# Attention with split operands in a mixed attention, recurrence and expert kernel

## The chip, the cores and the metric

The kernel runs on one core of one Trainium2 chip. The metric is device microseconds (us) of one execution. The engines are named as in the profile: PE (TensorE, matmuls), PEld (its weight loads, which overlap PE), DVE (VectorE), ACT (ScalarE), POOL (GpSimd) and SP (SyncE, which issues nearly all transfers).

## The reference

One layer over 1024 tokens of width 1024. Two mixers work on the same projected input, and a mixture of experts follows. What the change touches is the attention mixer (8 heads, keys of 64 + 32 dimensions, values of 64) and where the output of the other mixer, a recurrence, is kept.

```python
def causal_attention(q, k, v):                      # blocks of 128 queries
    scores = jnp.einsum('bqhd,bkhd->bhqk', qb, k, preferred_element_type=jnp.float32) * scale
    scores = jnp.where(k_pos[None, :] <= q_pos[:, None], scores, -jnp.inf)
    probs = jax.nn.softmax(scores, axis=-1).astype(v.dtype)
    return jnp.einsum('bhqk,bkhd->bqhd', probs, v)
...
    mla_o = mla_group(p[..., :MLA_IN], ...)         # attention, then an RMS norm
    rwkv_o, v_i = rwkv7_group(p[..., MLA_IN:], ...) # the recurrence
    mix = jnp.concatenate([mla_o, rwkv_o], axis=-1) @ w_o[i]
    x = layer_norm(DEEPNORM_ALPHA * x + (1.0 + gt1) * mix, ...)
    ffn = moe_ffn(h, ...)                           # 32 experts, top 4
```

All operands are float32.

## The kernel before

The program is one long list of instructions, laid out by a planner that simulates the time line and fixes the order of each engine's queue; every queue is then worked off in order. The stages follow one another, and the planner overlaps their edges.

1. **phase_a** normalizes and transposes the input. **phase_c** projects it, 18 blocks of 128 columns. Each block takes 16 matmul products in three passes: an operand x is kept as hi (x rounded to the format fp32r) and lo (x - hi), and `mm` (lines 187 to 195) adds hi·hi, hi·lo and lo·hi. `split` (line 202) makes the pair: ACT casts, DVE subtracts. In the second half of phase_c, for each p of 4, three recurrence blocks are projected (`shifted`), then the rotary part of the queries (`rotary`, every other p), the rest of queries and keys (`nope`) and two blocks of values. Each result goes from PSUM into a tile `stage` (three buffers of 128x1024) and from there by DMA into DRAM tensors q_d, k_d, kr_d, v_d and rkv_d. PSUM tiles of tag `sm` have four banks.
2. **mixers** interleaves 8 attention heads (`head`) with 8 recurrence units (`rwkv_unit`, two 64-wide heads and half the sequence each, in four stages). A head loads its queries Q (96x1024), keys K (96 rows) and, for two heads at a time, values `vp`; Q and K have two buffers, `vp` one. Then, for each block qb of 128 queries: one or two score products of up to 512 keys (line 889) in plain float32, a mask product (891), the maximum on DVE (892), the exponential on ACT (898), the division by the sum on ACT (902), transposes of the 128x128 blocks on PE (910), in groups of up to four into one PSUM bank `mt`, and a copy of each group into the tile `pt` (912: DVE for the first group, ACT for the second). Every second block, a product of the values with `pt` is put off until the next block's transposes (`pv`, lines 914 to 925): values are the stationary operand (128 keys x 64), `pt` the moving one (128 x 256), in plain float32; its result is in the same single bank `mt` and ACT copies it into oT. A plain float32 product is two matmul instructions in the trace.
   A unit ends with `self.dst[p][:, ts]` written by DVE (847), an SBUF tile that holds all recurrence outputs.
3. **mix** takes groups of 256 tokens: `mix_in` splits the recurrence output and the normalized attention output, `mix_mm` multiplies by w_o (recurrence rows 4 to 7 first), then come layer norm, router and gates. The tiles oT and dst are used again for the residual rows `y`.
4. **moe** runs 32 experts with streamed weights, all of them in split passes.

Of the kernel before, what the change touches and what calls it, by code (L numbers as in the profile page):

```python
# [10 lines left out]
F32 = mybir.dt.float32  # L11
# [8 lines left out]
P = 128  # L20
# [4 lines left out]
NH = 8  # L25
# [37 lines left out]
WBUF, SBUF = 5, 4  # L63
MODS = 2
# [97 lines left out]
class Build:  # L162
# [49 lines left out]
    def setup(self):  # L212
# [244 lines left out]
    def phase_c(self, st, keep, rw_stack):  # L457
# [54 lines left out]
        nc.sync.dma_start(self.kr_d, t1[0:32])  # L512
# [41 lines left out]
        def rotary(g):  # L554
# [21 lines left out]
        for p in range(4):  # L576
# [10 lines left out]
            for b in (2 * p, 2 * p + 1):  # L587
                pv = self.psum("sm", 4)
                self.mm(pv, kn[:, b * P:(b + 1) * P], uv)
                t = stage()[:, 0:512]  # L590
                S.copy(t, pv)
                nc.sync.dma_start(self.v_d[b], t)
            if p == EARLY_UNIT:
# [5 lines left out]
                self.unit(0)  # L599

# [56 lines left out]
    def rwkv_unit(self, u):  # L657
# [189 lines left out]
        V.tensor_mul(self.dst[p][:, ts], pg, o)  # L847
# [3 lines left out]
    def mla_setup(self, st):  # L851
# [3 lines left out]

        self.Q, self.K = ([kp.tile([P, T], F32, name=f"{n}{j}") for j in range(2)] for n in "QK")
        for t in self.Q + self.K:
            nc.gpsimd.memset(t[96:P], 0.0)
        for K in self.K:
            nc.sync.dma_start(K[64:96], self.kr_d)  # L860
# [5 lines left out]
        self.vp = None  # L866

    def head(self, h, oT):
# [4 lines left out]
        Q, K = self.Q[h % 2], self.K[h % 2]  # L873
        nc.sync.dma_start(Q[0:96], self.q_d[h])
        nc.sync.dma_start(K[0:64], self.k_d[h])
        if h % 2 == 0:
            self.vp = ap.tile([P, NB, P], F32, name="vp", bufs=1)
            nc.sync.dma_start(self.vp, self.v_d[:, :, h * 64:h * 64 + P].rearrange("b p c -> p b c"))
        v = self.vp[:, :, half]
        late = None  # L880
        for qb in range(NB):
            n = (qb + 1) * P
            ss, mx, sm = [], ap.tile([P, 2], F32, name="m"), ap.tile([P, 2], F32, name="smm")
            pr = ap.tile([P, T], F32, name="pr")
            for j, c in enumerate(range(0, n, 512)):
# [3 lines left out]
                mm(s, Q[:, qb * P:(qb + 1) * P], K[:, c:c + w], start=True, stop=not last)  # L889
# [14 lines left out]
            if i == 0:  # L904
                pt = ap.tile([P, NB, 256], F32, name="pt", bufs=2)
            for k0 in range(0, qb + 1, 4):
# [4 lines left out]
                eng = S.copy if k0 else V.tensor_copy  # L911
                eng(pt[:, k0:k1, i * P:(i + 1) * P], tp[:, 0:(k1 - k0) * P].rearrange("p (k q) -> p k q", q=P))

            def pv(nk=qb + 1, pt=pt, t=qb // 2):
                po = self.psum("mt", 1)
                if t == 0:
                    mm(po[half, 0:P], v[:, 0], pt[:, 0, 0:P], start=True, stop=True)
                    for k in range(2):
                        mm(po[half, P:256], v[:, k], pt[:, k, P:256], start=(k == 0), stop=(k == 1))
                else:  # L920

                    for k in [0, nk - 1] + list(range(1, nk - 1)):
                        sl = slice(P, 256) if k == nk - 1 else slice(0, 256)
                        mm(po[half, sl], v[:, k], pt[:, k, sl], start=(k == 0), stop=(k == nk - 2))
                S.copy(oT[half, t * 256:(t + 1) * 256], po[half, 0:256])
# [9 lines left out]
    def mixers(self, st, left, first, oT, dst):  # L935
# [4 lines left out]
        self.dst = dst  # L940
# [836 lines left out]
```

## Time and profile before

| | us |
|---|---|
| median of 3 runs | 2546.7 (2533.74 to 2546.89) |
| the profiled execution, its own time | 2529.01 |
| its span, first to last instruction | 2527.2 |
| PE busy in the span | 2316.8 (92%) |
| weight loads (PEld) busy | 1960.6 (78%) |
| DVE busy | 1991.1 (79%) |
| ACT busy | 1414.6 (56%) |
| POOL busy | 533.4 (21%) |
| mean granted TensorE clock | 0.953 of full speed |

Busy times are unions of instruction durations. A matmul's duration includes the time in which its pipeline fills and drains, so successive matmuls overlap, and PE can be "busy" while it takes in nothing new. How far apart matmuls start tells what one of them costs. Rows of waits give how long an engine sat idle before an instruction, and what ended that.

### The profile page before, as it was taken

Reading aid. Unit: us, or ns where it says so; the run is one execution under the profiler, and the core shown is the slowest. Engines: PE = TensorE matmul, PEld = TensorE weight load, DVE = VectorE, ACT = ScalarE, POOL = GpSimd, SP = SyncE. Lnnn points to the kernel's source line nnn. Section 1 sums busy time; section 2 is a strip of 40 time slices with the busy share of each in tenths; the row PEclk is TensorE's granted clock in tenths of the full one; section 3 lists DMA queues with packets and bytes.
Section 4 is the critical chain, followed back from the end, with each engine's and each line's share of the span. In section 5 each row is a group of like instructions: output and inputs, shape, how many; then the busy total and the mean of one; then the engine's idle time right before and its main releaser. Section 6 shows DMA issues by size and latency. Waiting matters only on the chain. (4 is left out here: it accounts for less than half of the span.)

```text
span 2527.2 us, 41955 instructions
## 1 busy us (share of the span) xinstructions
PE 2316.8 (92%) x15523; PEld 1960.6 (78%) x15523; DVE 1991.1 (79%) x3854; ACT 1414.6 (56%) x2357; POOL 533.4 (21%) x411
## 2 busy tenths in 40 slices
PE   6999989999999895999999999989999898989992
PEld 3777766776666784988988888989889888889981
DVE  7666456676765776987988888888979798888977
ACT  5333333454546233765766666666657576666764
POOL 1004222222213444110112121121202021211113
PEclk9999989999989995999999999999989999999996
DMA  6378542222112225976978878787969788887973
GB/s 261 117 255 287 178 108 49 52 48 66 43 37 80 98 87 195 347 290 232 341 284 304 316 285 332 283 304 276 346 225 336 281 304 300 291 309 289 326 275 148
DMA packets 167334, 567.79 MB, mean 225 GB/s; under 512 B 64617, under 2 KB 79738, under 8 KB 116821
## 3 DMA queue, kind: packets, MB, share of 16 engines
q1 hardware_dynamic: 155476, 524.63, 56.6%
q0 software_dynamic: 11216, 39.34, 6.0%
q8 instruction: 124, 2.03, 0.3%
q10 hardware_dynamic: 432, 1.09, 0.1%
q14 instruction: 86, 0.70, 0.1%
HBM read 508.22 MB, written 56.79 MB: 224 GB/s over the span
## 5 line engine op out<-in xcount | busy, mean ns | idle before, releaser
L204 DVE TENSOR_TENSOR wsl<-w,wsh 128x1024 fp32r<-128x1024 f32 x786 | 936.6, 1225 | 140.1 <-ACT wsh L203 139.0
L203 ACT CAST wsh<-w 128x1024 fp32r<-128x1024 f32 x786 | 782.6, 1047 | 337.5 <-PE acc L193 95.2
L1508 PE MATMUL acc<-xw,wsh 128*128 128x368 f32 (+7 forms) x1408 | 387.7, 359 | 19.0 <-DVE t L1513 11.1
L193 PE MATMUL acc<-wsh,xTl 128*128 128x256 f32 x1344 | 382.1, 285 | 0.3 <-DVE xTl L204 0.3
L191 PE MATMUL acc<-wsh,xTh 128*128 128x256 f32 x1344 | 381.1, 284 | 0.9 <-ACT xTh L203 0.9
L192 PE MATMUL acc<-wsl,xTh 128*128 128x256 f32 x1344 | 381.5, 284 | 0.0
L1510 PE MATMUL acc<-xw,wsl 128*128 128x184 f32 (+7 forms) x1408 | 341.5, 243 | 0.0
L1508 PEld LDWEIGHTS acc<-xw,wsh 128*128 128x128 f32 x1408 | 274.5, 195 | 22.6 <-issue 12.0
L1442 POOL DMA_INDIRECT y_d<-y,idx x42 | 132.1, 3146 | 710.0 <-DVE y L1434 612.5
L1510 PEld LDWEIGHTS acc<-xw,wsl 128*128 128x128 f32 x1408 | 279.0, 198 | 0.4
L192 PEld LDWEIGHTS acc<-wsl,xTh 128*128 128x128 f32 x1344 | 258.4, 192 | 3.8
L191 PEld LDWEIGHTS acc<-wsh,xTh 128*128 128x128 f32 x1344 | 258.3, 192 | 2.5 <-ACT xTh L203 1.3
L193 PEld LDWEIGHTS acc<-wsh,xTl 128*128 128x128 f32 x1344 | 258.2, 192 | 1.6 <-DVE xTl L204 0.8
L191 PE MATMUL acc<-wsh,uTh 128*128 128x512 f32 x512 | 203.2, 398 | 8.2 <-ACT uTh L203 8.2
L192 PE MATMUL acc<-wsl,uTh 128*128 128x512 f32 x512 | 202.7, 396 | 0.0
L193 PE MATMUL acc<-wsh,uTl 128*128 128x512 f32 x512 | 195.1, 406 | 0.9 <-DVE uTl L204 0.9
L1346 POOL DMA_INDIRECT xg<-h_d,idx x43 | 95.1, 2211 | 367.7 <-DVE gate L1338 232.6
L191 PE MATMUL sm<-hTh,wsh 128*128 128x512 f32 x288 | 116.5, 405 | 6.7 <-ACT wsh L203 2.0
L192 PE MATMUL sm<-hTl,wsh 128*128 128x512 f32 x288 | 117.1, 407 | 4.2 <-DVE hTl L345 3.1
L191 PEld LDWEIGHTS acc<-wsh,uTh 128*128 128x128 f32 x512 | 97.4, 191 | 29.4 <-ACT uTh L203 9.3
L193 PE MATMUL sm<-hTh,wsl 128*128 128x512 f32 x288 | 115.2, 400 | 0.0
L192 PEld LDWEIGHTS acc<-wsl,uTh 128*128 128x128 f32 x512 | 97.5, 190 | 18.9
(582 smaller groups left out, 4371.4 us busy)
## 6 DMA issues: line engine op xcount, KB each, us to landing
w<-in_w_dram SPq DMA_DIRECT2D x384, 1024.0 KB
aw<-in_ada_dram SPq DMA_DIRECT2D x34, 512.0 KB
w<-in_w_in_dram SPq DMA_DIRECT2D x18, 512.0 KB
aw<-in_ada_dram SPq DMA_DIRECT2D x7, 1024.0 KB
rkv_d<-stage SPq DMA_DIRECT2D x12, 512.0 KB
xt<-in_x_dram SPq DMA_DIRECT2D x8, 512.0 KB
xr<-in_x_dram SPq DMA_DIRECT2D x8, 512.0 KB
xr_d<-xr SPq DMA_DIRECT2D x8, 512.0 KB
```

Source lines behind the costliest of these rows:

```text
L191: mm(out, a.hi, b.hi, start=start, stop=False)
L192: mm(out, a.hi, b.lo, start=False, stop=False)
L193: mm(out, a.lo, b.hi, start=False, stop=stop)
L203: (hi_eng or self.nc.scalar.copy)(dst.hi, src)
L204: (lo_eng or self.nc.vector).tensor_tensor(dst.lo, src, dst.hi.bitcast(F32), ALU.subtract)
L1346: nc.gpsimd.indirect_dma_start(out=xg[0:n], out_offset=None, in_=self.h2_d, in_offset=bass.IndirectOffsetOnAxis(ap=idx[0:n, 0:1], axis=0))
L1442: nc.gpsimd.indirect_dma_start(out=self.y_d, out_offset=bass.IndirectOffsetOnAxis(ap=idx[0:n, 0:1], axis=0), in_=y[0:n], in_offset=None, c ...
L1508: nc.tensor.matmul(acc[:, 0:2 * cap], w.hi[:, c], xw[:, k].rearrange("p a t -> p (a t)"), start=(k == 0), stop=False)
L1510: nc.tensor.matmul(acc[:, 0:cap], w.lo[:, c], xw[:, k, 0], start=False, stop=(k == KD - 1))
```

## The change

- Queries, keys and values are written to DRAM as hi and lo parts: q_d, k_d and kr_d get a leading dimension of 2, and v_d rows become 1024 wide. phase_c makes the parts, with `parted` for the rotary results (in the two stage tiles already held) and `split` into two stage tiles in `nope`, and into one tile of full width for the values.
- In the values' layout each head has 128 columns, hi beside lo, with the order turned for odd heads so that hi lies at the head's own half.
- Scores are three fp32r products per chunk instead of one float32 product. Q and K are loaded per half sequence (two Q tiles, three K buffers), and the rotary key rows for each head anew.
- The transposed weights are split (ACT cast, DVE subtraction, both from PSUM) instead of copied. The product with the values uses one 128-column stationary operand with both parts of the values, and two moving passes, hi and lo; the two halves of the result are added at the end (ACT copies one half to `ol`, DVE adds).
- The recurrence output goes to a DRAM tensor ro_d, and `mix_in` loads 256 tokens of it for each group. The SBUF tile dst goes.

```diff
+KBUF = 3
...
-        self.q_d = dram("q_d", [NH, 96, T])
-        self.k_d = dram("k_d", [NH, 64, T])
-        self.kr_d = dram("kr_d", [32, T])
-        self.v_d = dram("v_d", [NB, P, 512])
+        self.q_d = dram("q_d", [2, NH, 96, T])
+        self.k_d = dram("k_d", [2, NH, 64, T])
+        self.kr_d = dram("kr_d", [2, 32, T])
+        self.v_d = dram("v_d", [NB, P, 1024])
+        self.ro_d = dram("ro_d", [4, P, T])
@@ phase_c
-        nc.sync.dma_start(self.kr_d, t1[0:32])
+        for part, t in enumerate(self.parted(t1[0:32], t2[0:32])):
+            nc.sync.dma_start(self.kr_d[part], t)
@@ rotary
-            for j in range(4):
-                nc.sync.dma_start(self.q_d[4 * g + j, 64:96], t1[32 * j:32 * j + 32])
+            for part, t in enumerate(self.parted(t1, t2)):
+                for j in range(4):
+                    nc.sync.dma_start(self.q_d[part, 4 * g + j, 64:96], t[32 * j:32 * j + 32])
@@ nope
-            t = stage()
-            for h, pq in enumerate(project(name, p * P, srcs)):
-                S.copy(t[:, halves[h]], pq)
-            for h in range(2):
-                nc.sync.dma_start(dst[2 * p + h, 0:64], t[h * 64:h * 64 + 64])
+            th, tl = stage(), stage()
+            for sl, pq in zip(halves, project(name, p * P, srcs)):
+                self.split(Split(th[:, sl].bitcast(F32R), tl[:, sl].bitcast(F32R)), pq)
+            for part, t in enumerate((th, tl)):
+                for h in range(2):
+                    nc.sync.dma_start(dst[part, 2 * p + h, 0:64], t[h * 64:h * 64 + 64])
@@ values
-                t = stage()[:, 0:512]
-                S.copy(t, pv)
+                t = stage()
+                t4 = t.bitcast(F32R).rearrange("p (a n d) -> p a n d", a=4, n=4)
+                self.split(Split(t4[:, :, 0::3], t4[:, :, 1:3]), pv.rearrange("p (a n d) -> p a n d", a=4, n=2))
                 nc.sync.dma_start(self.v_d[b], t)
@@
+    def parted(self, x, hi):
+        self.split(Split(hi.bitcast(F32R), x.bitcast(F32R)), x)
+        return hi, x
@@ rwkv_unit
-        V.tensor_mul(self.dst[p][:, ts], pg, o)
+        V.tensor_mul(o, pg, o)
+        nc.sync.dma_start(self.ro_d[p, :, ts], o)
@@ mla_setup: the tiles Q and K, the memsets of rows 96 to 128 and the load of kr_d go
@@ head
-        Q, K = self.Q[h % 2], self.K[h % 2]
-        nc.sync.dma_start(Q[0:96], self.q_d[h])
-        nc.sync.dma_start(K[0:64], self.k_d[h])
-        if h % 2 == 0:
-            self.vp = ap.tile([P, NB, P], F32, name="vp", bufs=1)
-            nc.sync.dma_start(self.vp, self.v_d[:, :, h * 64:h * 64 + P].rearrange("b p c -> p b c"))
-        v = self.vp[:, :, half]
+        other = slice(0, 64) if h % 2 else slice(64, 128)
+        parts = lambda d: d.rearrange("a r t -> r a t")
+        Q, K = [], []
+        for sl in (slice(0, 512), slice(512, T)):
+            q, k = (ap.tile([96, 2, 512], F32R, name=n, bufs=b) for n, b in (("Q", 2), ("K", KBUF)))
+            nc.sync.dma_start(q.bitcast(F32), parts(self.q_d[:, h, :, sl]))
+            nc.sync.dma_start(k[0:64].bitcast(F32), parts(self.k_d[:, h, :, sl]))
+            nc.sync.dma_start(k[64:96].bitcast(F32), parts(self.kr_d[:, :, sl]))
+            for t, ts in ((q, Q), (k, K)):
+                ts.append(Split(t[:, 0], t[:, 1]))
+        v = ap.tile([P, NB, P], F32R, name="vp", bufs=1)
+        nc.sync.dma_start(v.bitcast(F32), self.v_d[:, :, h * P:(h + 1) * P].rearrange("b p c -> p b c"))
...
-                mm(s, Q[:, qb * P:(qb + 1) * P], K[:, c:c + w], start=True, stop=not last)
+                q, k = Q[qb // 4][:, qb % 4 * P:(qb % 4 + 1) * P], K[j][:, 0:w]
+                mm(s, q.hi, k.hi, start=True, stop=False)
+                mm(s, q.hi, k.lo, start=False, stop=False)
+                mm(s, q.lo, k.hi, start=False, stop=not last)
...
-                pt = ap.tile([P, NB, 256], F32, name="pt", bufs=2)
+                pt = self.split_tile(ap, [P, 6 + qb % 4, 256], f"pt{qb % 4}", bufs=1)
...
-                eng = S.copy if k0 else V.tensor_copy
-                eng(pt[:, k0:k1, i * P:(i + 1) * P], tp[...])
+                self.split(pt[:, k0:k1, i * P:(i + 1) * P], tp[...])
             def pv(nk=qb + 1, pt=pt, t=qb // 2):
                 po = self.psum("mt", 1)
+                def prod(k, sl, start, stop):
+                    mm(po[:, sl], v[:, k], pt.hi[:, k, sl], start=start, stop=False)
+                    mm(po[:, sl], v[:, k], pt.lo[:, k, sl], start=False, stop=stop)
...
-                        mm(po[half, sl], v[:, k], pt[:, k, sl], start=(k == 0), stop=(k == nk - 2))
-                S.copy(oT[half, t * 256:(t + 1) * 256], po[half, 0:256])
+                        prod(k, slice(P, 256) if k == nk - 1 else slice(0, 256), k == 0, k == nk - 2)
+                ol = ap.tile([P, 256], F32, name="ol", bufs=1)
+                S.copy(ol[half], po[other, 0:256])
+                V.tensor_tensor(oT[half, t * 256:(t + 1) * 256], po[half, 0:256], ol[half], ALU.add)
@@ mix_in, with ro a tile of 128x4x256 for group 0 and a slice of the new tile ys for the others
+        self.nc.sync.dma_start(ro, self.ro_d[:, :, ts].rearrange("j p t -> p j t"))
         for j in range(4):
-            self.split(mt[4 + j], ro[j][:, ts])
+            self.split(mt[4 + j], ro[:, j])
```

## Rows read from the trace of the kernel before

**Rows 1.** Stages; each engine's busy us with (x) instructions, granted clock, DMA share.

```profile
core 0: us, PE busy (x) PEld busy (x) DVE busy (x) ACT busy (x) POOL busy (x), PEclk, DMA share, GB/s
...
190.00:342.00 152.00, 144.83 (x634) 112.67 (x632) 79.13 (x99) 54.99 (x86) 53.33 (x30) 0.99 0.62 213
342.00:400.00 58.00, 47.85 (x325) 33.46 (x326) 42.61 (x149) 24.44 (x58) 12.29 (x16) 0.82 0.39 93
400.00:690.00 290.00, 283.98 (x2527) 202.53 (x2527) 201.79 (x679) 145.79 (x337) 71.74 (x114) 0.97 0.21 49
690.00:816.00 126.00, 116.85 (x959) 79.23 (x957) 72.94 (x233) 61.93 (x140) 32.92 (x39) 0.93 0.19 52
...
985.00:2527.00 1542.00, 1413.94 (x9684) 1296.38 (x9684) 1336.21 (x2142) 992.59 (x1514) 268.24 (x108) 0.96 0.80 293
```

**Rows 2.** Time line of PE between two busy units: start, duration of the run.

```profile
565.68 1.73 PE L924 MATMUL mt<-pt,vp 128*64 128x256 f32 x8
567.34 0.88 PE L750 MATMUL s<-rx,bk 64*128 64x64 f32 x6
...
570.70 1.02 PE L686 MATMUL s<-wdad,a 64*128 64x512 f32 x2
571.56 0.77 PE L750 MATMUL s<-rx,bk 64*128 64x64 f32 x6
...
572.59 0.60 PE L910 MATMUL mt<-csts,pr 128*128 128x128 f32 x4
573.03 0.95 PE L624 MATMUL s<-csts,oc 128*128 128x2 f32 x8
```

**Rows 3.** Time line of PE in the experts, fp32r products.

```profile
1100.94 0.40 PE L1455 MATMUL acc<-bs,pick 128*128 128x512 f32 x1
1101.17 0.28 PE L191 MATMUL acc<-wsh,xTh 128*128 128x256 f32 x1
...
1103.93 0.28 PE L193 MATMUL acc<-wsh,xTl 128*128 128x256 f32 x1
```

**Rows 4.** Attention products by line: duration min/median/max ns, starts, forms.

```profile
L889 PE MATMUL ms<-K,Q x192: 275/592/1220, 349.0 to 792.1; 128*128 128x512 f32 x96, 128*128 128x128 f32 x32, 128*128 128x256 f32 x32, 128*128 128x384 f32 x32
...
L924 PE MATMUL mt<-pt,vp x288: 272/379/686, 377.1 to 809.9; 128*64 128x256 f32 x120, 128*64 128x128 f32 x24
...
L919 PE MATMUL mt<-pt,vp x32: 272/272/273, 366.6 to 779.4; 128*64 128x128 f32 x32
...
L917 PE MATMUL mt<-pt,vp x16: 272/274/323, 366.3 to 778.9; 128*64 128x128 f32 x16
```

**Rows 5.** Copies out of bank mt by line, duration min/median/max ns.

```profile
L912 DVE COPY pt<-mt x64: 275/676/692, 361.9 to 804.7; 128x512 f32<-128x512 f32 x40, 128x128 f32<-128x128 f32 x8, 128x256 f32<-128x256 f32 x8, 128x384 f32<-128x384 f32 x8
L912 ACT COPY pt<-mt x32: 266/419/587, 375.1 to 806.2; 128x128 f32<-128x128 f32 x8, 128x256 f32<-128x256 f32 x8, 128x384 f32<-128x384 f32 x8, 128x512 f32<-128x512 f32 x8
```

**Rows 6.** Groups by line: a split out of PSUM, weight loads of both widths.

```profile
L192 PEld LDWEIGHTS acc<-wsl,xTh 128*128 128x128 f32 x1344 | 258.4, 192 | 3.8
...
L924 PEld LDWEIGHTS mt<-pt,vp 128*64 128x64 f32 x288 | 37.0, 140 | 21.6 <-issue 3.5 <-ACT pt L912 1.5 <-ACT pr L898 0.8
...
L204 DVE TENSOR_TENSOR xTl<-tr,xTh 128x512 fp32r<-128x512 f32 x42 | 28.3, 683 | 42.6 <-ACT xTh L203 42.6
...
L203 ACT CAST xTh<-tr 128x512 fp32r<-128x512 f32 x42 | 24.2, 585 | 74.4 <-PE tr L1357 73.4
```

**Rows 7.** Waits in the mixers: total us, times, longest.

```profile
ACT pr L898 <- PE mt L910: 44.2, 21, 4.6
```

**Rows 8.** Waits in the late projections.

```profile
ACT stage L591 <- DMA q_d<-stage: 6.2, 3, 3.2
...
ACT stage L440 <- DMA v_d<-stage: 2.8, 1, 2.8
```

**Rows 9.** Time line of PE at the first scores.

```profile
348.95 2.90 PE L889 MATMUL ms<-K,Q 128*128 128x128 f32 x6 [3.41 <-DMA K<-k_d]
```

**Rows 10.** Time line at the start of the mix.

```profile
816.48 0.79 PE L191 MATMUL mm<-wo4h,mt4h 128*128 128x512 f32 x1 [2.78 <-ACT mt4h L203]
```

More of the change, by code (lines that the diff above doesn't have):

```diff
@@ L854, in mla_setup @@
         self.ap = self.pool(st, "ap", bufs=2, side="right")
[L856 to L860, printed above, removed]
         self.nmask = kp.tile([P, P], BF16, name="nmask")
@@ L882, in head @@
             n = (qb + 1) * P
-            ss, mx, sm = [], ap.tile([P, 2], F32, name="m"), ap.tile([P, 2], F32, name="smm")
+            ss, ms = [], ap.tile([P, 4], F32, name="m")
+            mx, sm = ms[:, 0:2], ms[:, 2:4]
             pr = ap.tile([P, T], F32, name="pr")
@@ L910, in head @@
                     nc.tensor.transpose(tp[:, (k - k0) * P:(k - k0 + 1) * P], pr[:, k * P:(k + 1) * P], self.ident)
[L911 to L912 removed]
+                self.split(pt[:, k0:k1, i * P:(i + 1) * P], tp[:, 0:(k1 - k0) * P].rearrange("p (k q) -> p k q", q=P))
             def pv(nk=qb + 1, pt=pt, t=qb // 2):
                 po = self.psum("mt", 1)
+                def prod(k, sl, start, stop):
+                    mm(po[:, sl], v[:, k], pt.hi[:, k, sl], start=start, stop=False)
+                    mm(po[:, sl], v[:, k], pt.lo[:, k, sl], start=False, stop=stop)
                 if t == 0:
[L917 removed]
+                    prod(0, slice(0, P), True, True)
                     for k in range(2):
[L919 removed]
+                        prod(k, slice(P, 256), k == 0, k == 1)
                 else:
                     for k in [0, nk - 1] + list(range(1, nk - 1)):
[L923 to L925 removed]
+                        prod(k, slice(P, 256) if k == nk - 1 else slice(0, 256), k == 0, k == nk - 2)
+                ol = ap.tile([P, 256], F32, name="ol", bufs=1)
+                S.copy(ol[half], po[other, 0:256])
+                V.tensor_tensor(oT[half, t * 256:(t + 1) * 256], po[half, 0:256], ol[half], ALU.add)
             if i == 0 and late:
@@ L933, in head, with mixers @@
         yield
-    def mixers(self, st, left, first, oT, dst):
+    def mixers(self, st, left, first, oT):
         heads = ExitStack()
-        self.dst = dst
         go = self.unit
@@ L975, in mixers @@
             self.nc.scalar.activation(self.g1p, self.g1p, AF.Copy, bias=1.0)
-            self.pm = self.mix_mm(self.mix_in(oT, dst, 0))
+            self.pm = self.mix_mm(self.mix_in(oT, 0, self.pool(last, "r0", side="right").tile([P, 4, 256], F32, name="r0")))
             self.xs = self.mix_add(0, self.pm)
@@ L996, in mix_weights, with mix_in @@
                     self.split(self.wo[k][:, sl], w, lo_eng=self.nc.gpsimd)
-    def mix_in(self, oT, ro, g):
+    def mix_in(self, oT, g, ro):
         W = 256
@@ L1034, in mix_add, with mix @@
         return out
-    def mix(self, left, outer, oT, ro):
+    def mix(self, left, outer, oT):
         nc, tc = self.nc, self.tc
@@ L1042, in mix @@
             xp = self.pool(st, "xp", side="right")
+            self.ys = (self.oT, xp.tile([P, 4, T], F32, name="ys"))
             self.L, self.L2 = (xp.tile([P, NB, NE], F32, name=n) for n in ("L", "L2"))
@@ L1095, in mix @@
             for g in range(4):
-                mt = self.mix_in(oT, ro, g + 1) if g < 3 else None
+                mt = self.mix_in(oT, g + 1, self.ys[1][:, :, (g + 1) * 256:(g + 2) * 256]) if g < 3 else None
                 ys += [self.residual(wp, 2 * g + b, xs[b], rows, rw, rb) for b in range(2)]
@@ L1742, in tile_hybrid_mla_rwkv7_moe @@
             ro = b.pool(st, "ro", side="right")
-            b.ro = [ro.tile([P, 4, T], F32, name=n) for n in ("oT", "dst")]
-            oT, dst = ([t[:, j] for j in range(4)] for t in b.ro)
+            b.oT = ro.tile([P, 4, T], F32, name="oT")
+            oT = [b.oT[:, j] for j in range(4)]
             left = ExitStack()
-            b.mixers(st, left, first, oT, dst)
+            b.mixers(st, left, first, oT)
         with ExitStack() as s2:
             b.ps = b.pool(s2, "pl", space=PSUM)
-            b.mix(left, ctx, oT, dst)
+            b.mix(left, ctx, oT)
             b.banks = {}
```

3 lines of the change are left out of this document (1 added, 2 removed).

## The prediction

> **What bounds the kernel now.** I read the windows first, by stage [rows 1]. The experts take 1542 of 2527 us, and the change has nothing there. It touches the late projections (190 to 342 us), the mixers (342 to 816) and the first step of the mix. In the mixers' steady stretch (400 to 690) the reader is to see four numbers: PE 283.98 of 290 us busy, DVE 201.79 (70%), ACT 145.79 (50%), DMA share 0.21. PE is the fullest, but a matmul's duration holds its fill and drain, so 98% need not mean that matmuls are as dense as they can be. The time line decides that: the start of one run of products to the start of the next is what the run costs PE. Two float32 instructions of 512 columns take 0.86 us (570.70 to 571.56), 0.43 each; eight of 256 columns with the values take 1.66 (565.68 to 567.34), 0.21 each; four transposes of 128 columns take 0.44, 0.11 each [rows 2]. These sit close behind each other there, with no gap of PE that I could give to anything else. So in this stretch matmul work removed is time removed, as far as nothing else gets longer. The late projections are PE's too: 7.2 us idle of 152 [rows 1]. The heads run from 349.0 to 809.9 [rows 4], 57.6 us a head, each beside one recurrence unit.
>
> **What fp32r passes cost.** In the experts 24 passes of 256 columns start within 2.76 us, 0.12 apart, and one of 512 takes 0.23 [rows 3]. Per column that is a quarter of a float32 product (two instructions) for 512 columns (0.23 against 0.86) and 0.12 against 0.42 for 256.
>
> **Scores.** By the counts [rows 4], one head has 24 score instructions: 12 of 512 columns and 4 each of 384, 256 and 128. Before: 12 x 0.43 + 4 x 0.32 (in between) + 4 x 0.21 + 4 x 0.11 = 7.7 us. After, three passes: 18 x 0.23 + 6 x 0.17 + 6 x 0.12 + 6 x 0.12 = 6.6 us. No row has an fp32r pass of 128 columns; it lies between 0.06 (half of 256 columns) and 0.12 (no gain at all), and I take 0.12, because the transposes, as narrow, stand at 0.11.
>
> **Products with the values.** 288 + 32 + 16 instructions over 8 heads are 42 a head: five in six of the 36 are 256 wide, so 30 wide and 12 narrow [rows 4]. Before 30 x 0.21 + 12 x 0.11 = 7.6 us. After, two passes with 128 stationary columns instead of 64: 30 x 0.12 + 12 x 0.12 = 5.0 us. Together 3.7 us a head less, **29 us** for eight heads; 38 if the narrow passes take 0.06.
>
> **Weight loads.** The stationary operand of the values gets twice as wide: 140 ns becomes 192 [rows 6]. I cost that at nothing, because the experts' 0.12 us passes each have a load of 192 ns that lies under the pass before. If that cover were gone, a pass would cost 0.19: see the rivals.
>
> **DVE and ACT.** The first group of each block, now one DVE copy, gets an ACT cast ahead of the DVE pass: 0.27 + 0.37 + 0.48 + 5 x 0.59 = 4.1 us of ACT a head. The second group, now an ACT copy, gets a DVE pass: 0.28 + 0.42 + 0.55 + 0.68 = 1.9 us, and four additions of 256 columns make 1.6 more [rows 5]; a split of 512 columns out of PSUM, 585 and 683 ns, costs the same [rows 6]. DVE goes from 40 to 44 us of a head's 57.6, ACT from 29 to 33. Both stay below PE, so as work this is hidden behind PE's recurrence products.
>
> **The bank `mt`.** As a wait it is not hidden for certain. Transposes and value products share one bank, and PE takes its queue in order: when a group is not yet split, the transposes behind it wait, and all recurrence products queued behind them. A group of four holds the bank for 0.44 us of transposes and 0.68 of copy now, and then for 0.44 + 0.59 + 0.68. Over a head that is 4.1 + 1.9 + 1.6 = 7.6 us more, of which 2.5 come back from shorter value products. ACT already waits 44.2 us for these transposes, 21 times, with exponentials queued in front of it [rows 7]. The bounds are nothing, when the planner always has recurrence work to put between, and 7.6 us a head (61 in all), when each hold stops PE. I take 0.75 a head, **+6 us**: PE's idle time in the steady stretch is 6 us for five heads, 1.2 each [rows 1], and the hold grows by about a third, with a fuller DVE.
>
> **Late projections.** DVE gets some 20 us of subtractions (24 of 512 columns at 0.68, the rotary ones on top) in 152 us where it is busy for 79: hidden. 7.4 MB more are written; 213 GB/s at a share of 0.62 make 344 at full share, so 21 us of transfers, and the share rises to 0.76: hidden as well. What isn't free is the `stage` tile: `nope` takes two instead of one, eight more in all, and a tile comes free only when its DMA has landed. ACT waits for that now, 6.2 us in three waits and 2.8 in one [rows 8], while PE goes on thanks to the four `sm` banks. Bounds: nothing, and eight waits of 2.6 us on PE's path, 21. I take **+3**, nearer the low end, since 9 us of such waits now leave PE only 7.2 us idle for all causes together. SP issues 25 more stores there; the recurrence loads for unit 0 are queued behind them.
>
> **Loads of a head.** 0.9 MB become 2.1, at a DMA share of 0.21: hidden. The second halves of Q and K and the values can only be loaded when the head before is through with them. They are needed at the fifth block and after the third, so there is time; what stands behind them on SP are the recurrence's loads and stores of the next unit. The one wait of this kind on PE, at the first scores, is 3.41 us [rows 9]. I take nothing; bounds from 3.4 less (the memsets ahead of the first load go) to 3.4 us at each head, 27.
>
> **The trip through DRAM.** Unit 6's output, the last that group 0 of the mix needs, is written long before; only the load into its tile is new on the path, and that tile's memory is free when the last head is through. PE waits 2.78 us there now, for the cast of the same rows [rows 10]. I take **+2** (0 to 4, a load's wait as in rows 9). Unit 7's output is needed two groups later: nothing. The Trainium skill (DMA: Bandwidth & Descriptors, Anatomy of one DMA) gives each transfer about 2 us of fixed time, which for a store and a load is 4; by that, if the store counted as well, the sum would be 2 us worse, and no row here shows it.
>
> **The sum.** -29 + 6 + 3 + 2 = **-18 us**, against the profiled execution's own 2529.0 (its span and 1.8 around it). That execution is faster than all three runs, 17.7 below their median of 2546.7; taken from the median the forecast is **2528.7 us**.
>
> **Rivals.**
> 1. *The saving is kept whole, or the narrow passes are cheap*: -29 to -38, 2509 to 2518. For it: DVE and ACT have room. Against: the bank. 0.12.
> 2. *The bank eats it*: 2 to 4 us a head stay on PE, -29 + 5 + 16 to 32 = -8 to +8, about 2547. For it: ACT's wait in rows 7, and DVE, with 44 us of work in a head that would last some 55. 0.22.
> 3. *The bank decides, slower*: its holds become the longest thing in a head. Break-even is (29 - 5) / 8 = 3.0 us a head of the 7.6; above 4.6 the kernel is measurably slower, with all of it +37, 2584. Against: the value products and transposes have the recurrence's PE work, more than half of a head's, to hide behind. 0.19.
> 4. *Weight loads bind*: each fp32r pass costs at least its load, 0.19. Scores 18 x 0.23 + 18 x 0.19 = 7.6, values 42 x 0.19 = 8.0, no saving in either (15.6 against 15.3), so +2 + 11 = +13, 2560. It decides from about 0.18 on. Against: 0.12 with the same load [rows 3, 6]. 0.05. The Trainium skill (Perfetto Trace Analysis, Identifying the Most-Contended Engine) says that matmul busy time is a bad measure of PE and that the busy share of weight loads is a good one. By that rule the mixers have 30% of room now (202.53 of 290), and the change fills it: 10.5 us of loads a head become 15.0, 36 us more in all. The experts' stretch, 84% busy with loads, is where the 0.12 comes from, so the trace does not bear the rule out as a bound.
>
> **How the numbers follow.** The forecast's own case runs from -28 to -8 (2519 to 2539), chance 0.42. A change of under 0.5%, 12.7 us, can't be told from none here. Of the forecast's case 0.34 lies beyond it, with rival 1 that makes 0.46 faster. Its other 0.08 and rival 2 make 0.30 the same. Rivals 3 and 4 are 0.24 slower. The range 2508 to 2562 takes in the upper bound of the saving, rival 2, rival 4 and the near part of rival 3, and leaves out some 0.15.
>
> **What would show it.** Score passes 0.23 us apart at 512 columns, value passes 0.12 apart, with the heads' stretch (first scores to last value product) near 440 us instead of 461. PE idle before transposes and value products, ended by DVE or ACT passes out of `mt`, of about 2 us a head; 4 and more is rival 2, 6 and more rival 3. ACT waits for `stage` near 15 us in the late projections, with the first scores 3 us later than 349.0. Passes 0.19 apart would be rival 4. The forecast is wrong if the experts' stage changes, if the planner's new order leaves PE without recurrence work at a head's end, or if the load of the values comes late at each head.

## The result, and the profile after

The changed kernel takes 2638.8 us (median of four runs, 2633.3 to 2654.0) against 2545.7 of the kernel before in the same session: ratio 1.0413, 95% interval 1.0383 to 1.0443. It is 4.1% slower. The profiled execution takes 2633.3 us, with a span of 2631.5 against 2527.2.

The windows by stage answer to [rows 1] (columns as there): late projections, the mixers' steady stretch, all of the mixers up to the mix, the mix, the experts.

```profile
190.00:375.00 185.00, 151.93 (x639) 116.11 (x637) 97.77 (x137) 55.88 (x85) 50.56 (x31) 0.90 0.66 220
400.00:690.00 290.00, 266.74 (x2380) 210.97 (x2380) 201.40 (x639) 143.96 (x326) 66.16 (x100) 0.85 0.29 68
375.00:924.00 549.00, 482.58 (x3908) 381.04 (x3908) 350.57 (x1119) 265.02 (x607) 115.03 (x164) 0.80 0.27 67
924.00:1090.00 166.00, 143.03 (x703) 118.37 (x703) 122.97 (x280) 55.38 (x110) 73.24 (x72) 0.85 0.33 112
1090.00:2631.00 1541.00, 1416.84 (x9684) 1298.81 (x9684) 1333.11 (x2141) 990.26 (x1513) 262.31 (x108) 0.96 0.80 293
```

The mixers of the kernel before, cut in the same way:

```profile
349.00:816.00 467.00, 446.51 (x3790) 314.00 (x3790) 312.40 (x1040) 231.44 (x533) 113.78 (x163) 0.94 0.22 52
```

The starts and ends come from the attention's own lines in the changed kernel (duration min/median/max in ns, first and last start), beside [rows 4]:

```profile
L904 PE MATMUL ms<-K,Q x96: 223/498/1222, 374.9 to 896.4; 96*128 96x512 f32 x48, 96*128 96x128 f32 x16, 96*128 96x256 f32 x16, 96*128 96x384 f32 x16
L946 DVE TENSOR_TENSOR oT<-mt,ol x32: 404/420/429, 396.8 to 920.0; 64x256 f32<-64x256 f32 x32
```

The first scores come at 374.9 instead of 349.0 (+26). From there to the first product of the mix (924.3, before 816.5) it takes 549.4 us instead of 467.5 (+82). From there to the end it takes 1707 us instead of 1711 (-3). That is the whole difference of the spans, 104.3.

**Where the 82 us are.** PE's busy time times the granted clock is an estimate of the work at full rate: 446.5 x 0.94 = 420 us before, 482.6 x 0.80 = 386 after. By this estimate the saving did arrive, 34 us. But PE is idle for 66 us instead of 21 (+45), and loses 97 us to the lower clock instead of 27 (+70). -34 + 45 + 70 = 81; that the three make up the whole follows from how they are defined and proves nothing by itself. How far the estimate can be off shows in e14 below, where it finds 12 us more work than the passes that were added.

The time line of PE shows the passes at full clock, with [rows 2, 3] beside them: score passes of 512 columns 0.23 us apart (480.58 to 480.81), value passes of 256 columns 0.12 apart (479.55 to 479.67), and of the two value passes of 128 columns one takes 0.06 and the other 0.11 (479.21 to 479.27 to 479.38). Some 25 us later score passes of 256 columns stand 0.21 apart (506.32 to 506.53 to 506.75), nearly double the 0.12.

```profile
479.21 0.22 PE L934 MATMUL mt<-pt2h,vp 128*128 128x128 f32 x1
479.27 0.28 PE L935 MATMUL mt<-pt2l,vp 128*128 128x128 f32 x1
479.38 0.33 PE L934 MATMUL mt<-pt2h,vp 128*128 128x256 f32 x1
479.55 0.28 PE L935 MATMUL mt<-pt2l,vp 128*128 128x256 f32 x1
479.67 0.28 PE L934 MATMUL mt<-pt2h,vp 128*128 128x256 f32 x1
...
480.24 0.50 PE L904 MATMUL ms<-K,Q 96*128 96x512 f32 x1
480.58 0.40 PE L905 MATMUL ms<-K,Q 96*128 96x512 f32 x1
480.81 0.39 PE L906 MATMUL ms<-K,Q 96*128 96x512 f32 x1
...
485.07 1.09 PE L816 MATMUL s<-gk,t 64*64 64x128 f32 x16 [1.04 <-DVE t L808]
...
493.63 0.69 PE L927 MATMUL mt<-csts,pr 128*128 128x128 f32 x2 [1.32 <-DVE pt0l L206]
...
506.32 0.41 PE L905 MATMUL ms<-K,Q 96*128 96x256 f32 x1
506.53 0.41 PE L906 MATMUL ms<-K,Q 96*128 96x256 f32 x1
506.75 0.33 PE L908 MATMUL ms<-nmask,identb 128*128 128x128 bf16 x1
```

Narrow windows of the same 30 us give the granted clock (the number behind POOL's): it falls to 0.50, the 1.2 GHz level, and is back at 1.00, 2.4 GHz, from 512 on.

```profile
488.00:492.00 4.00, 4.00 (x23) 3.16 (x23) 3.42 (x18) 1.50 (x2) 0.00 (x0) 0.77 0.00 0
492.00:496.00 4.00, 2.68 (x13) 2.48 (x13) 3.66 (x17) 0.00 (x0) 0.42 (x2) 0.50 0.27 33
500.00:504.00 4.00, 4.00 (x11) 2.05 (x11) 2.71 (x10) 1.55 (x2) 0.00 (x0) 0.50 0.01 2
504.00:508.00 4.00, 4.00 (x14) 3.09 (x15) 1.95 (x4) 1.82 (x3) 0.00 (x0) 0.50 0.20 66
512.00:516.00 4.00, 4.00 (x33) 3.33 (x31) 1.96 (x5) 1.71 (x5) 2.05 (x4) 1.00 0.12 18
```

Ahead of the fall PE had stood still for 1.04 us, and in it for 1.32 more, this one until DVE was through with its pass out of `mt`. While the level is low, PE's records show it busy without a gap (500 to 508): work then takes about twice as long, and such time does not show as idle.

The waits of the heads' stretch (total us, times, longest) say where the new idle time begins. Before, ACT waited for PE at `mt` in [rows 7] and in two rows more, 111 us in all:

```profile
ACT oT L925 <- PE mt L924: 40.1, 18, 5.9
...
ACT pt L912 <- PE mt L910: 27.0, 15, 7.3
```

Now three rows make 156 us. DVE waits for ACT in the middle of a split, and PE for DVE's pass and, at the scores, for the exponentials that empty a score bank:

```profile
ACT pt0h L205 <- PE mt L927: 60.8, 28, 7.5
ACT ol L945 <- PE mt L935: 50.9, 20, 5.6
ACT pt2h L205 <- PE mt L927: 44.8, 29, 4.9
...
DVE oT L946 <- ACT ol L945: 24.2, 12, 4.3
DVE pt2l L206 <- ACT pt2h L205: 23.1, 22, 3.9
...
PE ms L904 <- ACT pr L915: 11.9, 11, 2.0
...
PE mt L927 <- DVE oT L946: 7.6, 7, 2.9
PE mt L927 <- DVE pt2l L206: 5.6, 5, 1.4
PE mt L927 <- DVE pt0l L206: 5.4, 6, 1.4
```

With its waits ahead of value products (5.5 us) PE stands for 24 us in all until a pass out of `mt` is through, where the kernel before had 2. That is the largest part of the 45 us of new idle time, but only about half of it.

In the late projections, where [rows 8] had 9 us of waits for `stage`, there are now 20 on ACT and 7 on DVE, and PE waits for DVE's pass out of an `sm` bank:

```profile
ACT stage L205 <- DMA k_d<-stage: 14.4, 5, 6.3
DVE stage L206 <- DMA q_d<-stage: 7.1, 2, 3.7
...
ACT stage L205 <- DMA q_d<-stage: 5.4, 3, 3.2
...
PE sm L193 <- DVE stage L206: 8.8, 3, 5.2
```

The loss is large in the first 30 us of that stretch, here before and after:

```profile
190.00:220.00 30.00, 26.88 (x109) 20.63 (x108) 19.93 (x23) 11.18 (x18) 16.49 (x7) 0.94 0.75 257
...
190.00:220.00 30.00, 16.65 (x51) 10.77 (x50) 21.76 (x24) 6.54 (x10) 17.12 (x7) 0.72 0.82 272
```

PE stands still there twice for some 5 us. The second stop has a `stage` tile behind it: the subtraction that PE waits for had itself waited 3.7 us for a store out of a tile, and DVE, busy for 4.5 of the 10 us from 200 to 210, was not short of time then:

```profile
203.89 1.87 PE L398 MATMUL md<-acc,ones 128*1 128x512 f32 x2 [4.92 <-DVE acc L392]
...
210.19 1.29 DVE L206 TENSOR_TENSOR stage<-sm,stage 128x512 fp32r<-128x512 f32 x2 [3.72 <-DMA q_d<-stage]
...
210.94 0.79 PE L193 MATMUL sm<-uvh,nrm2h 128*128 128x512 f32 x1 [5.18 <-DVE stage L206]
```

### The profile page after: what moved, and what is told of

Read it like the earlier page. It is cut to its first block, busy times and chain, and to the rows that moved or that the text cites. A ratio compares the mean times of both kernels' runs of the same rounds, so it can differ in the third digit from the quotient of the medians.

```text
span 2631.5 us, 42465 instructions
## 1 busy us (share of the span) xinstructions
PE 2357.6 (90%) x15619; PEld 2029.0 (77%) x15619; DVE 2038.5 (77%) x3945; ACT 1444.0 (55%) x2422; POOL 523.9 (20%) x407
```

## The experiments

All in one table: each kernel's time; its ratio to the kernel before, run in the same session (its medians lay between 2534 and 2546 us); and from the profile of one execution the start of the first scores, the time from there to the first product of the mix (mixers), PE's idle time in it, and its granted clock.

| run | us | ratio, 95% interval | first scores | mixers | PE idle | clock |
|---|---|---|---|---|---|---|
| before | 2545.7 | | 349.0 | 467.5 | 21.0 | 0.94 |
| after | 2638.8 | 1.0413, 1.0383 to 1.0443 | 374.9 | 549.4 | 66.7 | 0.80 |
| e1 scores only | 2572.8 | 1.0129, 1.0082 to 1.0175 | 375.3 | 484.6 | 31.9 | 0.91 |
| e2 values only | 2555.9 | 1.0073, 1.0048 to 1.0098 | 342.6 | 511.1 | 62.1 | 0.88 |
| e3 two mt | 2556.4 | 1.0071, 1.0041 to 1.0101 | 379.2 | 469.0 | 37.4 | 0.88 |
| e4 loads on POOL | 2658.3 | 1.0452, 1.0371 to 1.0533 | 381.7 | 580.6 | 73.4 | 0.76 |
| e5 before, two mt | 2531.2 | 1.0000, 0.9983 to 1.0017 | 348.0 | 471.8 | 25.2 | 0.93 |
| e6 evict, then split | 2615.9 | 1.0317, 1.0299 to 1.0336 | 376.7 | 535.8 | 50.9 | 0.82 |
| e7 stage 4 | 2610.0 | 1.0307, 1.0280 to 1.0335 | 375.6 | 529.1 | 65.6 | 0.84 |
| e8 = e3 + e7 | 2581.1 | 1.0186, 1.0152 to 1.0220 | 375.3 | 487.6 | 37.2 | 0.84 |
| e9 high part only | 2548.0 | 1.0045, 1.0015 to 1.0076 | 377.0 | 449.4 | 37.3 | 0.89 |
| e10 split at load | 2595.1 | 1.0212, 1.0158 to 1.0265 | 344.5 | 546.1 | 62.6 | 0.80 |
| e11 = e3 + e10 | 2537.7 | 0.9999, 0.9973 to 1.0024 | 346.9 | 471.9 | 36.4 | 0.87 |
| e12 = e2 + two mt | 2506.1 | 0.9894, 0.9843 to 0.9945 | 341.2 | 444.1 | 32.4 | 0.95 |
| e13 late evict | 2596.8 | 1.0220, 1.0178 to 1.0261 | 380.1 | 523.0 | 56.0 | 0.82 |
| e14 = e11 + 4th pass | 2567.9 | 1.0111, 1.0072 to 1.0150 | 347.6 | 496.5 | 27.6 | 0.87 |
| e15 = e12, order | 2510.9 | 0.9891, 0.9858 to 0.9923 | 343.3 | 449.4 | 31.4 | 0.94 |
| e16 = e15, order | 2509.5 | 0.9887, 0.9856 to 0.9918 | 342.6 | 447.7 | 36.6 | 0.96 |
| e17 = e10 + stores | 2603.3 | 1.0269, 1.0224 to 1.0314 | 349.5 | 546.3 | 58.1 | 0.78 |
| e18 = e10 + passes | 2605.7 | 1.0271, 1.0229 to 1.0314 | 358.7 | 545.0 | 68.1 | 0.82 |

A caution holds for all of it: the planner lays the queues out anew for each kernel. The edit of e7 lies in the projections alone, and yet made to the changed kernel it shortens the mixers by 20 us, and made to e3 (that is e8) it lengthens them by 19. Differences of that size in the mixers are not put down to an edit below. With it, no row tells the effect of an edit from that of the new order that comes with it.

### Which half of the change, and the bank

**e1** undoes the values' half (values float32, one copy out of `mt` per group, one load for two heads), **e2** the scores' half (Q, K and scores as before).

```diff
 e1
-  self.split(pt[...], tp[...])
+  (S.copy if k0 else V.tensor_copy)(pt[...], tp[...])
...
 e2
-  mm(s, q.hi, k.hi, ...); mm(s, q.hi, k.lo, ...); mm(s, q.lo, k.hi, ...)
+  mm(s, Q[:, qb * P:(qb + 1) * P], K[:, c:c + w], start=True, stop=not last)
...
```

> Only the scores are split; the products with the values are float32 as before, with one copy out of the bank mt per group and the values loaded once for two heads. Bank theory (the split out of mt with its longer hold stops PE): the heads' stretch is no longer than before's 461 us, and the time is 2545 plus at most the 26 us by which the first scores came later, 2545 to 2571. Loads theory (Q and K in halves, which wait on SP for PE and hold the recurrence's loads up): most of the 84 us in the heads stays, 2600 or more. Staging theory for the late projections (two stage tiles per block of Q and K): the first scores stay near 370 us.

> Only the products with the values are split; Q, K and the scores are as before. Bank theory: the heads' stretch stays near 545 us and the time near 2615 (without the later first scores). Loads theory: the values' load for each head is the only late one left, at most a third of the 84 us, 2575 or less. Staging theory: the first scores are back within 8 us of 349.

The late first scores belong to the scores' half (375.3 and 342.6). In the mixers the scores' half makes 17 us more than before and the values' half 44; together 61 of the 82. PE's idle time goes with the values: 62 us in e2, nearly the 67 of the whole change, and 32 in e1. Neither run is where the bank theory had put it: e1's heads took 472 us, 11 more than it allows, and e2's 511 where it said 545. e2's time, 2556 us, even fits the bound of the loads theory (2575), though its heads, 50 us above before's, do not (at most a third of the 84).

**e3** gives `mt` a second bank, taken from the scores. **e5** does the same to the kernel before.

```diff
-  s = self.psum("ms", 3)[:, 0:w]
+  s = self.psum("ms", 2)[:, 0:w]
-  tp = self.psum("mt", 1)          # po alike
+  tp = self.psum("mt", 2)
```

> The whole change, with two banks for mt and two instead of three for the scores (ms). Bank theory: a split no longer stops the transposes behind it; at least half of the 84 us in the heads comes back, 2600 or less, with the granted clock of the heads' stretch above 0.88. Loads theory: no change from 2639 beyond 10 us. If the scores' three banks are worth as much, it is slower than 2639.

> The kernel before, with the same trade of banks as e3 (two for mt, two for the scores). Bank theory (the change's longer hold of mt is what costs): before loses little to the bank, so 2531 to 2547 here, within 8 us of 2539. If it is 30 us or more below before, the single bank cost both kernels and the 83 us of e3 are not the change's own.

In the changed kernel the trade is worth 80 us of the mixers' 82 (549.4 to 469.0); in the kernel before nothing (ratio 1.0000). Three more pairs below differ by this trade alone: e7 and e8 (41 us of the mixers), e10 and e11 (74), e2 and e12 (67). All are beyond the 20 us of the caution. So the single bank costs these four kernels, in which the weights are split in two parts, and not the one before. The waits of e3 go with it:

```profile
ACT ol L945 <- PE mt L935: 22.2, 14, 5.8
ACT pt2h L205 <- PE mt L927: 21.8, 17, 3.7
...
ACT pt0h L205 <- PE mt L927: 9.9, 10, 3.1
...
PE mt L927 <- DVE pt2l L206: 1.6, 1, 1.6
```

ACT's 156 us have become 54, and PE's 18.6 us ahead of the transposes less than 2. PE's wait for the exponentials at the scores falls from 11.9 us to 1.0, though the scores have a bank less. The Trainium skill (Perfetto Trace Analysis, Matmuls) says that independent groups of matmuls should go round through different PSUM banks, so that emptying one overlaps the next group's products; e3 agrees with it for the changed kernel, and e5 shows for the one before that the rule can be worth nothing. The windows of e3 also show what the planner makes of it, heads first and 50 us of recurrence behind them, at a clock of 0.60 (e5 has the same):

```profile
379.20:798.10 418.90, 393.35 (x3574) 319.59 (x3574) 324.31 (x1059) 243.52 (x571) 94.21 (x139) 0.91 0.31 72
798.10:848.20 50.10, 38.27 (x312) 28.04 (x312) 16.20 (x41) 15.57 (x28) 21.00 (x25) 0.60 0.36 107
```

**e9** keeps one bank and drops the low part of the weights, so a group leaves the bank in one copy. **e6** keeps both parts and one bank, but empties the bank in one copy and splits from SBUF.

```diff
 e9
-  self.split(pt[...], tp[...])
+  (S.copy if k0 else V.tensor_copy)(pt[...], tp[...])
-  mm(po[:, sl], v[:, k], pt.lo[:, k, sl], start=False, stop=stop)
 e6
-  self.split(pt[...], tp[...])
+  raw = pr[:, k0 * P:k1 * P]
+  (S.copy if k0 else V.tensor_copy)(raw, tp[...])
+  self.split(pt[...], raw, lo_eng=nc.gpsimd)
```

> The change without the low part of the weights: each group leaves the one bank mt in a single copy (DVE or ACT, as before), and each value product is one pass instead of two. So part of the computation is left out: the low part of the softmax weights. Hold theory (the second pass out of the bank): the heads' stretch falls from 545 to 460 or less, since the hold is that of before and PE does 2.5 us less a head, and the time to 2565 or less. If the bank's hold is not it, only the 20 us of PE work come off, and the time is 2610 to 2625.

> The whole change with one bank for mt, but each group of transposes leaves the bank in one copy, as before, into columns of pr that are no longer needed, and is split from there, ACT making the high part and GpSimd the low part. Hold theory (two passes out of the bank, one after the other, keep it taken): the heads' stretch is 490 us or less instead of 545 and the time 2590 or less. If the longer chain from the transposes to the value products costs as much as the hold, or DVE and ACT work does, the time stays within 15 us of 2639.

e9 takes 100 us off the mixers, far more than the 20 us of PE work that it leaves out, as the hold theory has it. e6 takes 14 off, within what a new order does, though each group of transposes leaves the bank in one copy as before; its time, 2615.9 us, is 26 above what the theory asked for. So the hold of a group of transposes alone is not the whole of it. In e6 as in e9 the value products still leave the bank in two passes. In e6 PE still waits at `mt` for the copies (DVE 5.6, ACT 5.3 us) and for `oT` (5.6), while the way from a transpose to its value product is longer by a GpSimd pass. What e6 and the changed kernel share, and e9 doesn't, is that way in three steps with the value products in two passes behind it. Which of these keeps the one bank taken is left open.

### The loads

**e4** issues each head's loads from GpSimd's queue.

```diff
-  nc.sync.dma_start(q ..., k ..., v ...)
+  nc.gpsimd.dma_start(q ..., k ..., v ...)
```

> The whole change, with the loads of each head (Q, K, the rotary rows, the values) issued from GpSimd's queue instead of SP's. Loads theory (a load that waits for PE holds up the recurrence's round trips behind it on SP): at least half of the 84 us comes back, 2600 or less, unless GpSimd's own work is now held up by the same waits. Bank theory: within 15 us of 2639.

It is 20 us slower than the changed kernel, not faster. So it is not the place of the loads in SP's queue that costs; and in the changed kernel's mixers PE waits for a load of Q, K or the values only once, 5.3 us ahead of the first scores.

### The late projections

**e7** has four `stage` tiles; to make room, the sigmoid rows take theirs from `stage` too and the raw weight blocks have one buffer. **e10** stores Q and K whole, as before, and splits them in each head. **e13** copies each block out of `sm` once and splits it from `stage`, without DVE. **e17** and **e18** add to e10 the change's stores alone and its passes alone.

```diff
 e7
-  stage = lambda: wp.tile([P, T], F32, name="stage", bufs=3)
+  stage = lambda: wp.tile([P, T], F32, name="stage", bufs=4)
...
 e10
-  nc.sync.dma_start(q.bitcast(F32), parts(self.q_d[:, h, :, sl]))
+  nc.sync.dma_start(q[:, 1].bitcast(F32), self.q_d[h, :, sl])
+  self.split(Split(q[:, 0], q[:, 1]), q[:, 1].bitcast(F32), lo_eng=nc.gpsimd)      # K alike
...
 e13
-  self.split(Split(th[:, sl], tl[:, sl]), pq)
+  S.copy(tl[:, sl], pq); self.split(Split(th[:, sl], tl[:, sl]), tl[:, sl], lo_eng=nc.gpsimd)
...
 e17, against e10
+  nc.sync.dma_start(q2_d ..., t ...)                                               # each store of q_d, k_d again
...
 e18, against e10
+  V.tensor_tensor(tl[:, halves[h]], pq, t[:, halves[h]], ALU.subtract)             # tl: a second stage tile
...
```

> The whole change, with four stage tiles instead of three in the late projections (the sigmoid rows take theirs from stage too, and the raw weight blocks have one buffer, to make room). Staging theory (two tiles per block of Q and K, each held until its store has landed): the first scores start at 358 or earlier instead of 375, and the time falls by 12 to 26 us, 2613 to 2627. If it is DVE's subtractions or the stores' bandwidth that makes the projections later, the first scores stay within 5 us of 375.

> The whole change with one bank for mt, but Q, K and the rotary rows go through DRAM whole, as before, and each head splits its Q and K after the load, ACT making the high part and GpSimd the low part in place. Late-projections theory (the splits of Q and K out of the sm banks, with DVE in the way, are what makes the first scores late): the first scores start at 350 or earlier, and the time falls by 20 to 32 us, 2607 to 2619. If the values' split or something else made them late, they stay near 375. The splits at load add about 4 us of ACT and 5 us of GpSimd to each head: if those hold the first scores of each head up, the heads' stretch grows beyond 545.

> The whole change, with only the late projections' splits of Q and K altered: each half of a block leaves its sm bank in one ACT copy and is split from the stage tile, high part by ACT, low part by GpSimd; the rotary rows' low parts go to GpSimd too. DVE is out of it. Bank theory for the late projections (the second pass out of an sm bank waits in DVE's queue, 73% busy there, and PE for the bank): the first scores start at 358 or earlier instead of 375. If it is the number of passes and stores for each block, or the stage tiles, they stay at 370 or later, and the time within 15 us of 2639.

> e10, with every store of Q and K in the late projections issued a second time, into other DRAM tensors that nothing reads: the stores of the change without its splits. Stores theory (a stage tile comes free only after twice the stores, and SP issues twice as many): the first scores start at 365 or later instead of e10's 344.5, and the time is some 20 to 30 us above 2595. Passes theory: the first scores stay at 352 or earlier.

> e10, with a DVE subtraction of each half of a Q or K block out of its sm bank, behind the ACT copy, into a second stage tile, and one on the rotary rows, with nothing stored of it: the passes and the second stage tile of the change without its stores. Passes theory (the second reader holds the sm bank and fills DVE): the first scores start at 360 or later instead of 344.5. Stores theory: 352 or earlier. If both this and e17 stay at 352 or earlier, the two together make the 26 us and neither alone.

The first scores tell. Splitting after the load brings them back (344.5); so it is the splits of Q and K in this stage, with their stores, that cost. A fourth tile does not (375.6), although the waits of ACT and DVE for a store out of `stage` fall from 32 us to 15.5: so they are not, by their sum, what sets the first scores, and the staging theory falls as I put it. With 15.5 us left and two other buffers changed, e7 doesn't clear the tile altogether. One copy out of the bank without DVE does not bring them back either (380.1: the bank theory of this stage falls as I put it; PE then waits for ACT's copy instead). e13 is still 42 us faster than the changed kernel, where its other theory allows 15; 26 of these are in the mixers, where it changes nothing. The stores alone make 5 us, the passes with their tile 14. What is missing to 26 or 30 would come only with both; the stop at 210.94 above, where a subtraction waits for a store, is of that kind. PE's row for the passes says how they cost:

```profile
PE sm L193 <- DVE stage L574: 9.4, 3, 6.9
```

One subtraction that comes late holds an `sm` bank, and PE stands for up to 6.9 us. In all, e10 is 44 us faster than the changed kernel: 30 from the first scores, the rest elsewhere. The splits at load cost the mixers nothing that shows (546.1 against 549.4).

### Both causes out, and the clock

**e8** is e3 with e7, **e11** is e3 with e10. **e14** adds to e11 a fourth score pass, low times low.

```diff
 e14, against e11
-  mm(s, q.lo, k.hi, start=False, stop=not last)
+  mm(s, q.lo, k.hi, start=False, stop=False)
+  mm(s, q.lo, k.lo, start=False, stop=not last)
```

> e3 and e7 together. If the bank and the stage tiles are the two causes, the gains add: 2556 less 12 to 26 us, 2530 to 2544, level with before or slightly below. If the recurrence's own chain sets the end of the mixers once the heads are shorter, the earlier start still counts, and the mix starts near 825 instead of 848.

> e3 and e10 together: both causes taken out. If the gains add, 2556 less 20 to 32 us, 2524 to 2536, so level with before or up to 0.5% faster. If e3's gain was the planner's luck with one order, as e8's 2581 hints, it lands anywhere from 2530 to 2580.

> e11 with a fourth score pass (low times low): 2.2 us more PE work a head by pitches of 0.23, 0.17 and 0.12, 17 us in all. Work theory (PE's time is its passes): the time rises by 10 to 20 us from 2538. Clock theory (e11 does less PE work than e12 but at a granted clock of 0.87 against 0.95 in the mixers, because denser PE work is what keeps the clock up): the clock of the mixers rises and the time stays within 8 us of 2538 or falls.

e8 is 25 us slower than e3: the gains of e3 and e7 do not add, since e7's was not what I took it for. e11 has both causes out and stands level with before (0.9999), 101 us below the changed kernel. So taking out the two causes takes away the loss, and the change's saving is still not to be seen.

The windows of the mixers of e11, e14 and e12 (values only, two banks, next section):

```profile
346.90:818.80 471.90, 435.54 (x3886) 349.53 (x3886) 346.15 (x1098) 274.01 (x629) 155.67 (x197) 0.87 0.25 63
```

```profile
347.60:844.10 496.50, 468.92 (x3983) 377.09 (x3983) 350.86 (x1103) 274.84 (x629) 159.53 (x197) 0.87 0.24 60
```

```profile
341.20:785.30 444.10, 411.69 (x3811) 308.82 (x3809) 350.45 (x1116) 259.50 (x600) 118.03 (x165) 0.95 0.27 65
```

e11 does less PE work than e12 by the estimate (435.5 x 0.87 = 379 against 391) with about the same idle time (36 against 32), and takes 28 us longer: by the estimate the lower clock costs 36 us more and the work 12 less. e14 shows that this is not for want of PE work: 17 us more of it by the passes added (29 by the estimate), the least idle time of the kernels with split scores (27.6), the same 0.87, and 30 us more time. The clock theory as I put it there falls. Why the three-pass scores go with a lower clock is open.

### A version that beats both

**e12** is e2 with two banks. **e15** puts the last recurrence step ahead of head 7, **e16** also the recurrence's steps ahead of the halves of each head.

```diff
 e15
+  go(7)
   list(self.head(7, oT[3]))
   heads.close()
-  go(7)
 e16, in the loop over the heads
   go(u + 2)
+  go(u)
   next(head)
-  go(u)
+  go(u + 1); go(u)
   next(head)
-  go(u + 1); go(u)
```

> e2 (only the products with the values are split) with two banks for mt and two for the scores. Bank theory: the 49 us by which e2's heads are longer than before's come back, and the time is 2505 to 2535, below before if the cheaper value products (2.6 us a head) count. If the bank is no part of it, within 10 us of e2's 2556.

> e12 with the last step of recurrence unit 7 written ahead of head 7 instead of behind it. Tail theory (after the last head, 51 us of the recurrence alone at a granted clock of 0.66): up to half of the tail moves under head 7, and the time falls from 2506 to 2480 to 2495. If PE's total work sets the end, within 8 us of 2506.

> e15 with the recurrence's steps written ahead of the halves of a head in every turn of the loop as well. Tail theory: the recurrence keeps up with the heads, the tail is under 25 us and the time 2470 to 2495. If the heads now wait for PE behind the recurrence, slower than e15.

e12 takes 2506.1 us, ratio 0.9894 (0.9843 to 0.9945): faster than both kernels, with 67 us less in the mixers than e2. e15 and e16 are no faster, against the tail theory. In e15 the stretch behind the last head stays at 51 us. In e16 it shrinks to 22 and the mixers stay at 448: the tail was the planner's order, and it cost nothing.

## Why the prediction was wrong

**The step that failed is the bank.** I put +6 us on `mt`, the hold being 7.6 us a head longer, as PE's idle time of 1.2 us a head [rows 1] would grow with it by a third. (A third of 1.2 is 0.4 a head, not the 0.75 I took; the rest stood on a fuller DVE, without a row.) Two banks give back 80 us, 10 a head, and 41 to 74 in the three other pairs. Two things were wrong with it. The idle time that I scaled was not the bank's: e5 shows that the bank cost the kernel before nothing, so there was no proportion to take. And the upper bound, 61 us, priced a stop of PE at its own length; the sum had no term for the clock. By the estimate above, 45 us more are idle time and 70 more are work at the lower clock, with 34 less of work. The Trainium skill (TensorE: Matmul & The Clock Gate, A second HAM failure mode: psum-queue depth-cycling) tells of a kernel whose PE is briefly idle between groups of matmuls again and again, so that the clock swings between half and full; the rows of 488 to 516 us show such a swing, though whether an idle time set it off, and which, no run here tells.

**The late projections** I put at +3, at most 21. They cost 26. I had called DVE's subtractions hidden because DVE was busy for 79 us of 152, and the waits for `stage` nearly so because PE had four `sm` banks to go on with. But in the first 30 us of that stretch PE is busy for 17 us instead of 27, with two stops of some 5 us: one for a product of the modulation rows, behind DVE, which had been busy without a gap until 203.8, and one at an `sm` bank, behind the subtraction that waited for a store. DVE's share, 20 us of the 30 before and 22 now, tells only of the first. The stage is an average of a tight beginning and a loose end, and much of the loss fell into the beginning. e18 (14 us) and e17 (5) say that it is passes first, stores next; that the rest is the two together is the remainder and was not run alone.

**Right were** the passes (0.23 and 0.12 us, so rival 4 fell), the PE work that went away, 34 us by the estimate (29 to 38; the value passes of 128 columns take 0.06 and 0.11 in turn, between the two values that I gave), the experts, and the loads of a head (e4 gives no sign of a cost). The trip through DRAM, where I had put +2, cost nothing: from the start of the last pass into oT to the first product of the mix it takes 4.3 us, before 6.2.

**The rival that happened** is the third, the bank decides, to which I gave 0.19 and at most 2584 us. That the bank decides was right. Its price was not, for want of the clock, and the 26 us ahead of it were no part of it. Nor would the sign that I gave for it, PE's idle time at `mt`, have told it: that is 24 us, 3 a head, between the 2 of the forecast and the 4 of rival 2, and not 6. And why the bank decides is not the hold of the groups alone, as e6 shows.

**Not settled:** why e6's short hold did not help; why three-pass scores lower the clock with two banks; whether PE's idle time is what lowered the clock; how much of each single difference is the planner's order, some 20 us in the mixers.

## What to carry to other kernels

Before an eviction out of PSUM becomes two passes on two engines, count the banks that its producer has: here a second one was worth 41 to 80 us in four kernels with split weights and nothing in the one before, and the idle time seen in the old kernel said nothing about it. A saving of PE work is worth its size only while PE keeps its clock, so a forecast with new waits on PE's path needs a term for it: here 45 us of new idle time went with 70 us at the lower level, and in e2 41 with 27. Read what is to hide new work in the narrowest stretch in which it falls due, not over the stage, and follow a wait on to what the awaited engine was itself waiting for; and of a change in two halves, measure each alone: here the values' half with a second bank is worth 1.1%, and the scores' half takes it away.

## What the hardware showed that I had not expected

PE's granted clock stayed at 0.50 for some 20 us (from about 490 to 510) while its records show one gap, of 1.3 us. Over the mixers the clock went from 0.94 to 0.80, which by the estimate cost more (70 us) than the idle time itself (45). It did not follow the idle time alone: e2 has 62 us of it at 0.88, e10 63 us at 0.80, e14 28 us at 0.87, e12 32 us at 0.95.
